# The scale half of layer 1's modulation is summed during the output projection of layer 0, not during the Hyena groups

## The chip, the cores and the metric

The kernel runs on one core of a Trainium2 chip. Its time is the device time of one execution in microseconds (us), and a version is compared by the median of several runs. TensorE (PE) multiplies, VectorE (DVE) and ScalarE (ACT) do elementwise work, GpSimd (POOL) does elementwise work and issues some DMAs, and SyncE's queue (SP) issues most DMAs. Each engine runs its own instructions strictly in the order in which they were written; a waiting instruction holds everything behind it.

## The reference

Two layers over 512 latent and 256 context tokens of width 1024. Each layer normalizes its input, applies a modulation that depends on a conditioning vector (shift, scale, gate), mixes and adds the gated result:

```
m = silu(c) @ ada_w[l] + ada_b[l]          # 3072 wide: shift, scale, gate
h = rms_norm(x, norm_g[l]) * (1 + scale) + shift
layer 0:  proj = h @ w_in;  u = x1 * v;  y = irfft(rfft(u) * rfft(k)) + u * d
          branch = (y * x0 * silu(z)) @ w_out      # 2048 channels, Hyena
layer 1:  branch = attention(h)                    # 16 query heads, 4 key heads
x = x + gate * branch
```

Latent tokens use the vector `c`, context tokens the vector `c_ctx`: the modulation is needed for two streams, numbered 0 and 1.

## The kernel before, in words

Layer 0 works on 8 groups g of two chunks of 128 channels. Per group, four convolutions per chunk (x1, v, z, x0) are matmuls whose fp32 weights arrive by DMA in a ring of three 512 KB buffers, tag `stg`; ACT splits off the high part `whi` (L121), POOL, or near the end DVE, the low part `wlo` (L122), and PE multiplies (L465 to L470). DVE turns the products in PSUM into the convolved rows `cvx` and `cvv` (L512 to L515); the pair of PSUM banks of a convolution is used again two convolutions later. Then come the transposed input `utl` (L543), spectra and their products `ab` (L560: `ab411a` is group 4, chunk 1, second part), whose reading of `pu` frees the PSUM bank in which PE next forms a lag of the next group's filter, `pk` (L379, L380; DVE takes it up at L382), and the inverse transform (`y`, L625 to L629, after ACT's `qs`, L624).

The modulation is a side job. `ada_pairs` makes five items for each 512 columns: four steps, each a 512 KB load `adas` (L189) into the same ring `stg` and one multiply-add per stream and half (L196 for the first, else L198) into the accumulators `adaacc`, and a last item that sums over partitions on PE and adds the bias (`adap`, L169 and L172), or for a gate writes rows. A list `todo` holds the items, and `ada_next` takes the next one. Its places: the letters `a` of `steps`, and two in the list handed to `x0_stage(g, 1, ...)`. These items stand as calls between the convolution's eight k steps, so that their position in each engine's order is fixed by the order in which the code is written.

After the groups comes layer 0's output projection in two halves of the 1024 output columns. `out_part(half, ...)` goes over 16 channel tiles `cht`: a weight pair every second tile (again `stg`, with `whi`/`wlo` or `whx`/`wlx`), the rows `yf` by a POOL DMA, split into `yh` (ACT) and `yl` (DVE, L752), and 18 matmuls into six PSUM banks `po`. `out_finish` adds the last two or four tiles, scales with the gate (`res`, L770) and so frees bank g of the six, which the other half needs next. `tables` loads a rope table into `stg` (`ropeq`, `ropek`, L809), multiplies it on POOL (L818, L822) and writes it to DRAM (`t_scrq`, `t_scrk`, L823, by SP). `make_gsc(1)` forms layer 1's column scale from the scale half; its first use is `turn_rows`, after the second half's `out_finish`. Attention, from about 1000 us, ends the kernel.

Of the kernel before, what the change touches and what calls it, by code (L numbers as in the profile page):

```python
# [11 lines left out]
F32 = mybir.dt.float32  # L12
F32R = mybir.dt.float32r
# [6 lines left out]
P = 128  # L20
# [32 lines left out]
def hybrid_kernel(ctx: ExitStack, tc: tile.TileContext, x, c, ctxt, c_ctx, norm_g, ada_w, ada_b,  # L53
# [20 lines left out]
    def f(ap):  # L74
        return ap.bitcast(F32)
# [99 lines left out]
    def make_gsc(l):  # L175
        for s in range(2):
            V.scalar_tensor_tensor(gsc[l][:, s * 8:(s + 1) * 8], ada[l][:, s * 24 + 8: s * 24 + 16], 1.0,
                                   vb[:, l * 8:(l + 1) * 8], ALU.add, ALU.mult)

    def ada_pairs(l, o0, streams, accp):  # L180

        nm = f"_{l}_{o0}"
        accs = []

        def step(kk):
            st = wp.tile([P, 1024], F32, tag="stg", name=f"adas{nm}_{kk}", bufs=NST)
            sv = st.rearrange("p (k o) -> p k o", k=2)
            src = ada_w[l][kk * 2 * P:(kk + 1) * 2 * P, o0:o0 + 512]
            nc.sync.dma_start(sv, src.rearrange("(k p) o -> p k o", p=P))  # L189
            for n_, s in enumerate(streams):  # L190
                if kk == 0:
                    accs.append(accp.tile([P, 512], F32, tag="adaacc", name=f"adaacc{nm}_{s}", bufs=NACC))
                for k in range(2):
                    sc = sil[:, s * 8 + kk * 2 + k:s * 8 + kk * 2 + k + 1]
                    if kk == 0 and k == 0:
                        V.tensor_scalar(accs[n_], sv[:, k, :], sc, None, ALU.mult)  # L196
                    else:
                        V.scalar_tensor_tensor(accs[n_], sv[:, k, :], sc, accs[n_], ALU.mult, ALU.add)  # L198

        def gate_rows():  # L200
            st = wp.tile([P, 1024], F32, tag="stg", name=f"adag{nm}", bufs=NST)
            nc.sync.dma_start(st[0:1, 0:512], ada_b[l:l + 1, o0:o0 + 512])
            for n_, s in enumerate(streams):
                pt = axt(f"adag{nm}_{s}")
                TE.matmul(pt[0:1, :], ones[:, 0:1], accs[n_], start=True, stop=True)
                V.tensor_tensor(st[0:1, 512:1024], pt[0:1, :], st[0:1, 0:512], ALU.add)
                nc.sync.dma_start(g_scr[f"{l}{s}"][:, o0 - 2 * DM:o0 - 2 * DM + 512], st[0:1, 512:1024])

        last = gate_rows if o0 >= 2 * DM else lambda: ada_cols(l, o0, 512, accs, streams, nm)
        return [lambda kk=kk: step(kk) for kk in range(4)] + [last]  # L210
# [391 lines left out]
    def x0_stage(g, j, items):  # L602
        i = 2 * g + j
        x0 = conv(i, f"x0_{i}", items)
        V.tensor_tensor(x0, x0, szs0.pop(i), ALU.mult)
        gxs[i] = x0
# [24 lines left out]

    todo = []
    for l, o0, streams in ([(0, 2048 + o * 512, [0, 1]) for o in range(2)]
                           + [(1, o * 512, [0, 1]) for o in range(4)] + [(1, 2048 + o * 512, [0]) for o in range(2)]):
        todo += ada_pairs(l, o0, streams, hp)

    def ada_next():
        if todo:
            todo.pop(0)()
# [6 lines left out]
    def filter_items(g):  # L646
        if g >= 8:
            return []
        lags = []
        return [lambda: lags.extend(kfilter(g))] + [lambda i=i: lags[i]() for i in range(6)]  # L650
# [24 lines left out]
    for g in range(8):  # L675
        ks = [later(kdft, g, *k) for k in KSETS]
        kn = later(knorm, g)
        ya = [lambda: y_stage(g - 1, 0)] if g else []
        yb = [lambda: y_stage(g - 1, 1)] if g else []
        def slots(text):  # L680

            table = {"n": kn[0], "N": kn[1], "a": ada_next, "-": none, "y": lambda: [y() for y in ya],
                     "Y": lambda: [y() for y in yb]}
            for i in range(4):
                table["mpoc"[i]], table["MPOC"[i]] = ks[i]
            return [lambda w=w: [table[ch]() for ch in w] for w in text.split()]

        sl = [slots(text) for text in steps[g == 0]]
        ta = u_stage(g, 0, sl[0], sl[1])
        tb = u_stage(g, 1, sl[2], sl[3] + ta)  # L690
        if g == 0 and "u" in dbg:
            for j in range(2):
                nc.sync.dma_start(dbg["u"][j], us[j])
        z_stage(g, 0, sl[4] + tb)
        x0_stage(g, 0, spectra(g, 0))
        z_stage(g, 1, spectra(g, 1) + [none])
        x0_stage(g, 1, [none, ada_next] + filter_items(g + 1) + [ada_next])
    while todo:
        ada_next()
    make_gsc(1)  # L700
    p0.close()
    wp2 = ctx.enter_context(pool("wpipe2", side="right"))

# [142 lines left out]
    p1.close()  # L846
    p2 = ctx.enter_context(ExitStack())
    o2 = p2.enter_context(pool("rows"))
    out_part(0, range(EARLY, NCH), TA, {6: load_rows, 10: lambda: tables(at_q_g, "q")})
    for g in range(NG):  # L850
        out_finish(g, 0, TA)
    out_part(1, range(NCH), TB, {4: lambda: tab_.update(k=tables(at_k_g, "k"))})
    tabk = tab_["k"]
    load_half("k0", EH, 0, None, V)
    load_half("k0", EH, 1, more_w, G)
# [462 lines left out]
```

## Time and profile before

| | us |
|---|---|
| median of 3 runs | 1518.78 (1512.92 to 1520.66) |
| profiled execution | 1517.56 |
| its span in the trace | 1515.7, mean granted clock 0.983 |
| PE busy | 1455.5 (96%) |
| DVE busy | 1183.7 (78%) |
| ACT, POOL busy | 547.5 (36%), 513.9 (34%) |

The Hyena groups take about 60 to 840 us, layer 0's output projection 840 to 960, layer 1 the rest. A share of the whole span is a mean over these three. A row of the timeline tells when an instruction began and how long it took; a bracket at its end tells how long its engine stood idle before it and which instruction ended the wait. A row of the windows has, for each engine, its busy time in the stretch, then the granted TensorE clock as a part of 2.4 GHz, the DMA engines' busy share, and GB/s.

### The profile page before, as it was taken

To read this page: it belongs to the slowest core of one execution; us is meant where nothing else is said; L and a number is where in the kernel's file an instruction comes from. 1 tells how busy PE (TensorE), PEld (TensorE's weight loads), DVE (VectorE), ACT (ScalarE), POOL (GpSimd) and SP (SyncE) were. 2 spreads that over 40 slices of the span, in tenths; PEclk is the share of its full clock that TensorE was granted. 3 is DMA by queue.
4 is the path that set the end of the run, shared out by engine and by line. 5 is a ranking of instruction groups with operands and counts; after the bars stand their busy time and mean duration, and the time that the engine had idled before them with its cause. 6 is when DMAs were issued, how large, how long until landed. Compare 5 with 4: busy or idle time off the path is not lost.

```text
span 1515.7 us, 22866 instructions
## 1 busy us (share of the span) xinstructions
PE 1455.5 (96%) x8787; PEld 1263.9 (83%) x8787; DVE 1183.7 (78%) x2004; ACT 547.5 (36%) x1057; POOL 513.9 (34%) x449
## 2 busy tenths in 40 slices
PE   8998999989999999999999999999999999999998
PEld 1787987878878878789888787799998998998987
DVE  5769879889789888987969644575787878878886
ACT  3431322313223223223232334543545544544542
POOL 2462744626537354264464343121110000000005
PEclk9999999999999999999999999999999999999999
DMA  8612223232232232223233667246232212212111
GB/s 298 189 50 83 78 77 91 77 93 86 74 105 69 85 87 70 87 85 90 84 98 108 236 218 260 72 123 214 85 112 70 82 58 70 84 57 70 44 64 74
DMA packets 150783, 157.45 MB, mean 104 GB/s; under 512 B 6953, under 2 KB 122212, under 8 KB 150164
## 3 DMA queue, kind: packets, MB, share of 16 engines
q1 hardware_dynamic: 146324, 134.76, 28.7%
q0 software_dynamic: 4208, 20.72, 4.0%
q8 instruction: 69, 1.13, 0.3%
q10 hardware_dynamic: 144, 0.52, 0.1%
q14 instruction: 38, 0.31, 0.1%
HBM read 138.14 MB, written 17.84 MB: 103 GB/s over the span
## 4 chain that ended last, share of the span: by engine, by line
PE 60%; DVE 23%; issue 5%; POOL 5%; DMA 4%; ACT 2%; SPq 0%; POOLq 0%; ACTq 0%; DVEq 0%
PE po L70 4%; PE po L72 4%; PE po L71 4%; DVE adaacc L198 3%; PE et L1114 3%; DMA adas<-in_ada_w_dram 2%; PE px L70 2%; PE pz L70 2%; PE px L72 2%; PE pz L72 2%; PE px L71 2%; PE pz L71 2%; PE pq L70 2%; PE pq L72 2%; PE pq L71 2%
## 5 line engine op out<-in xcount | busy, mean ns | idle before, releaser
L122 POOL TENSOR_TENSOR wlo<-stg,whi 128x1024 fp32r<-128x1024 f32 x64 | 159.3, 2489 | 260.9 <-ACT whi L121 256.6
L121 ACT CAST whi<-stg 128x1024 fp32r<-128x1024 f32 x99 | 103.8, 1049 | 233.6 <-PE pcz L468 81.1
L873 POOL TENSOR_TENSOR r2q<-s2q,mhalf 128x2 f32<-128x2 f32 x32 | 23.4, 731 | 343.6 <-DVE s2q L871 332.4
L465 PE MATMUL plx<-h_hi,whi 128*128 128x512 f32 x248 | 104.1, 420 | 8.1 <-DVE cvx L515 8.1
L198 DVE SCALAR_TENSOR_TENSOR adaacc<-adas,sil,adaacc 128x512 f32<-128x512 f32 x98 | 102.8, 1053 | 10.9 <-DMA adas<-in_ada_w_dram 10.6
L1102 ACT ACTIVATE E<-sc,st 128x768 f32<-128x768 f32 x64 | 57.7, 902 | 126.9 <-DVE st L1100 114.1
L469 PE MATMUL plx<-h_hi,wlo 128*128 128x512 f32 x248 | 101.3, 409 | 0.0
L466 PE MATMUL plx<-h_lo,whi 128*128 128x512 f32 x248 | 101.3, 408 | 0.0
L467 PE MATMUL pcx<-hc_hi,whi 128*128 128x256 f32 x248 | 72.5, 292 | 4.7 <-DVE cvx L515 4.6
L1099 DVE TENSOR_REDUCE st<-sc 128x1 f32<-128x768 f32 x64 | 61.0, 953 | 17.5 <-PE sc L72 17.2
L468 PE MATMUL pcx<-hc_lo,whi 128*128 128x256 f32 x248 | 71.7, 289 | 0.0
L470 PE MATMUL pcx<-hc_hi,wlo 128*128 128x256 f32 x248 | 71.5, 288 | 0.0
L752 DVE TENSOR_TENSOR yl<-yf,yh 128x768 fp32r<-128x768 f32 x26 | 25.7, 990 | 51.9 <-ACT yh L751 51.8
L1119 DVE TENSOR_TENSOR ptl<-et,pth 128x768 fp32r<-128x768 f32 x64 | 61.1, 954 | 5.3 <-ACT pth L1118 4.0
L465 PEld LDWEIGHTS plx<-h_hi,whi 128*128 128x128 f32 x248 | 49.2, 198 | 18.7 <-issue 8.8
L467 PEld LDWEIGHTS pcx<-hc_hi,whi 128*128 128x128 f32 x248 | 49.2, 198 | 18.5 <-issue 4.9
L1118 ACT CAST pth<-et 128x768 fp32r<-128x768 f32 x64 | 51.1, 798 | 31.1 <-PE et L1114 31.0
L468 PEld LDWEIGHTS pcx<-hc_lo,whi 128*128 128x128 f32 x248 | 49.1, 198 | 11.3
L465 PE MATMUL plv<-h_hi,whi 128*128 128x512 f32 x120 | 49.4, 412 | 5.5 <-DVE cvv L515 5.5
L72 PE MATMUL po<-pth,kvt 128*128 128x256 f32 x192 | 54.1, 282 | 0.0
L71 PE MATMUL po<-ptl,kvt 128*128 128x256 f32 x192 | 54.0, 281 | 0.0
L70 PE MATMUL po<-pth,kvt 128*128 128x256 f32 x192 | 53.9, 281 | 0.0
(909 smaller groups left out, 5181.5 us busy)
## 6 DMA issues: line engine op xcount, KB each, us to landing
stg<-in_hy_w_in_dram SPq DMA_DIRECT2D x64, 512.0 KB
stg<-in_at_w_in_dram SPq DMA_DIRECT2D x40, 512.0 KB
adas<-in_ada_w_dram SPq DMA_DIRECT2D x32, 512.0 KB
yf<-y_scr POOLq DMA_DIRECT2D x32, 384.0 KB, 5.0
ad<-in_ada_w_dram SPq DMA_DIRECT2D x16, 512.0 KB
stg<-in_hy_w_out_dram SPq DMA_DIRECT2D x16, 512.0 KB
stg<-in_at_w_out_dram SPq DMA_DIRECT2D x16, 512.0 KB
dec<-in_k_dec_dram SPq DMA_DIRECT2D x48, 128.0 KB
```

What stands on the lines that cost most here:

```text
L70: TE.matmul(ps, lh, rh, start=first, stop=False)
L71: TE.matmul(ps, lh, rl, start=False, stop=False)
L72: TE.matmul(ps, ll, rh, start=False, stop=last)
L121: S.copy(hi, st)
L122: (lo_eng or lo_default[0]).tensor_tensor(lo, st, f(hi), ALU.subtract)
L198: V.scalar_tensor_tensor(accs[n_], sv[:, k, :], sc, accs[n_], ALU.mult, ALU.add)
L465: TE.matmul(pl, hi[:, k, :], h_hi[:, k, :], start=fi, stop=False)
L466: TE.matmul(pl, hi[:, k, :], h_lo[:, k, :], start=False, stop=False)
L467: TE.matmul(pc[:, 0:LC], hi[:, k, :], hc_hi[:, k, :], start=fi, stop=False)
L468: TE.matmul(pc[:, 0:LC], hi[:, k, :], hc_lo[:, k, :], start=False, stop=False)
L469: TE.matmul(pl, lo[:, k, :], h_hi[:, k, :], start=False, stop=la)
L470: TE.matmul(pc[:, 0:LC], lo[:, k, :], hc_hi[:, k, :], start=False, stop=la)
```

## The change

The ten items of layer 1's columns 1024 to 2047 (the scale) leave the list that the Hyena groups work off. The first of the two places in `x0_stage(g, 1, ...)` goes, and with it the filter's items move one place earlier there. The ten items are put into `todo` again after the groups: two are taken in the first half of the output projection, after tiles 12 and 14, eight in the second, after tiles 0 to 3 and 5 to 8. Their accumulators lie in another pool's buffer of three (`kst`). `make_gsc(1)` comes after them.

```diff
--- before.py
+++ after.py
@@ -189,7 +189,7 @@
                 if kk == 0:
-                    accs.append(accp.tile([P, 512], F32, tag="adaacc", name=f"adaacc{nm}_{s}", bufs=NACC))
+                    accs.append(accp(f"adaacc{nm}_{s}"))
@@ -631,8 +631,8 @@
     for l, o0, streams in ([(0, 2048 + o * 512, [0, 1]) for o in range(2)]
-                           + [(1, o * 512, [0, 1]) for o in range(4)] + [(1, 2048 + o * 512, [0]) for o in range(2)]):
-        todo += ada_pairs(l, o0, streams, hp)
+                           + [(1, o * 512, [0, 1]) for o in range(2)] + [(1, 2048 + o * 512, [0]) for o in range(2)]):
+        todo += ada_pairs(l, o0, streams, lambda n: hp.tile([P, 512], F32, tag="adaacc", name=n, bufs=NACC))
@@ -694,10 +694,9 @@
         z_stage(g, 1, spectra(g, 1) + [none])
-        x0_stage(g, 1, [none, ada_next] + filter_items(g + 1) + [ada_next])
+        x0_stage(g, 1, [none] + filter_items(g + 1) + [ada_next])
     while todo:
         ada_next()
-    make_gsc(1)
@@ -846,10 +845,17 @@
-    out_part(0, range(EARLY, NCH), TA, {6: load_rows, 10: lambda: tables(at_q_g, "q")})
+    for o in range(2, 4):
+        todo += ada_pairs(1, o * 512, [0, 1], lambda n: f(o2.tile([P, 512], F32R, tag="kst", name=n, bufs=3)))
+    out_part(0, range(EARLY, NCH), TA, {6: load_rows, 10: lambda: tables(at_q_g, "q"), 12: ada_next, 14: ada_next})
     for g in range(NG):
         out_finish(g, 0, TA)
-    out_part(1, range(NCH), TB, {4: lambda: tab_.update(k=tables(at_k_g, "k"))})
+    late = {i: ada_next for i in range(12)}
+    late[4] = lambda: tab_.update(k=tables(at_k_g, "k"))
+    out_part(1, range(NCH), TB, late)
+    while todo:
+        ada_next()
+    make_gsc(1)
```

Three places show how the order moves. The first is DVE's order in group 4, from the second piece of `utl` on, before:

```order
L543 TENSOR_TENSOR utl_4304<-ut_4_4636,uth_4303 128x2x128
L198 SCALAR_TENSOR_TENSOR adaacc_1024_0_4599<-adas_1024_1_4871,sil,adaacc_1024_0_4599 128x512
L560 TENSOR_TENSOR ab400a<-pu_0_0_4664,kt_4454 128x1024
L198 SCALAR_TENSOR_TENSOR adaacc_1024_0_4599<-adas_1024_1_4871,sil,adaacc_1024_0_4599 128x512
L560 TENSOR_TENSOR ab400b<-pu_1_0_4677,kt4m_4217 128x1024
L198 SCALAR_TENSOR_TENSOR adaacc_1024_1_4602<-adas_1024_1_4871,sil,adaacc_1024_1_4602 128x512
L584 TENSOR_TENSOR ab400a<-ab400a,ab400b 128x1024
L198 SCALAR_TENSOR_TENSOR adaacc_1024_1_4602<-adas_1024_1_4871,sil,adaacc_1024_1_4602 128x512
L569 TENSOR_TENSOR Y_0_0_4695<-ab400a 128x256
```

The same stretch of DVE's order after the change, from four rows ahead of `utl`:

```order
L198 SCALAR_TENSOR_TENSOR adaacc_512_0_4530<-adas_512_2_4923,sil,adaacc_512_0_4530 128x512
L198 SCALAR_TENSOR_TENSOR adaacc_512_1_4533<-adas_512_2_4923,sil,adaacc_512_1_4533 128x512
L198 SCALAR_TENSOR_TENSOR adaacc_512_0_4530<-adas_512_2_4923,sil,adaacc_512_0_4530 128x512
L198 SCALAR_TENSOR_TENSOR adaacc_512_1_4533<-adas_512_2_4923,sil,adaacc_512_1_4533 128x512
L543 TENSOR_TENSOR utl_4273<-ut_0_4598,uth_4272 128x4x128
L543 TENSOR_TENSOR utl_4273<-ut_4_4605,uth_4272 128x2x128
L560 TENSOR_TENSOR ab400a<-pu_0_0_4633,kt_4428 128x1024
L560 TENSOR_TENSOR ab400b<-pu_1_0_4646,kt4m_4186 128x1024
L584 TENSOR_TENSOR ab400a<-ab400a,ab400b 128x1024
L569 TENSOR_TENSOR Y_0_0_4664<-ab400a 128x256
```

The multiply-adds that stood between the products now stand ahead of `utl`, all four of one step together; from `utl` to `ab411a` DVE's order holds six of them before and none after. Over the eight groups the number between `utl` and `ab{g}11a` goes from 4, 5, 5, 6, 6, 6, 4, 4 to 1, 3, 0, 0, 0, 2, 2, 0, and the number from there to the next group's first `cvx` from 4, 6, 6, 5, 5, 5, 2 to 4, 4, 4, 0, 4, 2, 2.

The second place is SP's order in the output projection, from the q table's gain on, before (`stg` with `in_hy_w_out` are weight pairs):

```order
L813 DMA tbk<-in_at_q_g_dram 128x128
L118 DMA stg_8126<-in_hy_w_out_dram 128x2x512
L823 DMA t_scrq<-tbk 128x1024
L118 DMA stg_8220<-in_hy_w_out_dram 128x2x512
L813 DMA tbk<-in_at_k_g_dram 128x128
L118 DMA stg_8274<-in_hy_w_out_dram 128x2x512
L118 DMA stg_8328<-in_hy_w_out_dram 128x2x512
L809 DMA ropek<-in_k_rope_dram 128x1024
L823 DMA t_scrk<-tbk 128x1024
L118 DMA stg_8398<-in_hy_w_out_dram 128x2x512
```

The same stretch of SP's order after, from the first modulation load on:

```order
L189 DMA adas_1024_0_8026<-in_ada_w_dram 128x2x512
L822 DMA t_scrq<-tbk 128x1024
L118 DMA stg_8058<-in_hy_w_out_dram 128x2x512
L189 DMA adas_1024_1_8070<-in_ada_w_dram 128x2x512
L118 DMA stg_8158<-in_hy_w_out_dram 128x2x512
L812 DMA tbk<-in_at_k_g_dram 128x128
L189 DMA adas_1024_2_8188<-in_ada_w_dram 128x2x512
L189 DMA adas_1024_3_8218<-in_ada_w_dram 128x2x512
L118 DMA stg_8224<-in_hy_w_out_dram 128x2x512
L189 DMA adas_1536_0_8289<-in_ada_w_dram 128x2x512
L118 DMA stg_8297<-in_hy_w_out_dram 128x2x512
```

Five loads through the ring now stand ahead of `ropek`, which with `t_scrk` follows directly on the last row, and the sixth, `adas_1536_1`, comes right behind `t_scrk`.

The third place is DVE's order where the first half's banks are freed (`res_0` to `res_5`), before:

```order
L770 TENSOR_TENSOR res_2_8172<-po_2_7636,gate_7889 128x512
L770 TENSOR_TENSOR res_3_8184<-po_3_7637,gate_7889 128x512
L770 TENSOR_TENSOR res_4_8196<-po_4_7638,gate_7889 128x512
L770 TENSOR_TENSOR res_5_8208<-po_5_7639,gate_7889 128x512
L752 TENSOR_TENSOR yl_3_8306<-yf_3_8304,yh_3_8305 128x768
```

The same stretch after:

```order
L769 TENSOR_TENSOR res_2_8110<-po_2_7560,gate_7813 128x512
L198 SCALAR_TENSOR_TENSOR adaacc_1536_0_8291<-adas_1536_1_8367,sil,adaacc_1536_0_8291 128x512
L769 TENSOR_TENSOR res_3_8122<-po_3_7561,gate_7813 128x512
L198 SCALAR_TENSOR_TENSOR adaacc_1536_0_8291<-adas_1536_1_8367,sil,adaacc_1536_0_8291 128x512
L769 TENSOR_TENSOR res_4_8134<-po_4_7562,gate_7813 128x512
L769 TENSOR_TENSOR res_5_8146<-po_5_7563,gate_7813 128x512
```

Two multiply-adds of the load `adas_1536_1` now stand ahead of `res_3` and `res_4`.

## Rows read from the trace of the kernel before

**Rows 1.** Windows: two stages (stretch; length; engines' busy us; PEclk; DMA; GB/s).
```profile
60.00:840.00 780.00, 735.12 (x4420) 646.02 (x4419) 667.27 (x892) 225.65 (x371) 388.80 (x285) 0.97 0.29 86
840.00:960.00 120.00, 119.02 (x538) 97.69 (x539) 55.32 (x60) 42.36 (x59) 39.27 (x61) 1.00 0.67 228
```
**Rows 2.** Waits of PE in 60 to 840 us: total, times, longest.
```profile
PE plx L465 <- DVE cvx L515: 8.1, 4, 2.7
PE plv L465 <- DVE cvv L515: 5.5, 5, 3.4
PE pcx L467 <- DVE cvx L515: 4.6, 2, 3.4
PE pk L379 <- DVE ab411a L560: 3.2, 1, 3.2
...
PE pk L379 <- DVE ab211a L560: 1.7, 1, 1.7
PE pu L71 <- DVE utl L543: 1.6, 1, 1.6
```
**Rows 3.** Timeline of PE: end of the first wait listed for `pk`.
```profile
535.86 0.64 PE L379 MATMUL pk<-w4h,h 128*128 128x512 f32 x1 [3.15 <-DVE ab411a L560]
```
**Rows 4.** Windows: PE right after four of these waits.
```profile
338.00:341.40 3.40, 3.38 (x18) 2.91 (x19) 3.40 (x5) 0.00 (x0) 0.00 (x0) 1.00 0.12 36
535.80:539.20 3.40, 3.34 (x10) 2.79 (x11) 3.40 (x5) 0.00 (x0) 0.00 (x0) 0.53 0.11 32
570.30:573.70 3.40, 3.31 (x11) 2.86 (x12) 3.40 (x5) 0.00 (x0) 0.00 (x0) 0.52 0.06 7
822.90:829.70 6.80, 6.25 (x21) 5.42 (x22) 6.76 (x8) 0.87 (x2) 3.02 (x2) 0.51 0.46 154
```
**Rows 5.** The instructions on L198 in 60 to 840 us: ns min/median/max.
```profile
L198 DVE SCALAR_TENSOR_TENSOR adaacc<-adas,sil,adaacc x98: 617/752/3377, 64.0 to 810.0; 128x512 f32<-128x512 f32 x98
```
**Rows 6.** Window with the instructions of L198 alone, group 4 (DVE busy us, count).
```profile
508.50:534.40 25.90, 6.40 (x6) 1.00 0.30 89
```
**Rows 7.** Timeline of DVE, groups 4 and 5.
```profile
507.55 1.02 DVE L543 TENSOR_TENSOR utl<-ut,uth 128x512 fp32r<-128x512 f32 x2 [2.51 <-ACT uth L542]
...
514.70 1.77 DVE L198 SCALAR_TENSOR_TENSOR adaacc<-adas,sil,adaacc 128x512 f32<-128x512 f32 x1
...
520.03 1.24 DVE L198 SCALAR_TENSOR_TENSOR adaacc<-adas,sil,adaacc 128x512 f32<-128x512 f32 x1 [0.62 <-DMA adas<-in_ada_w_dram]
...
534.50 1.21 DVE L560 TENSOR_TENSOR ab411a<-pu,kt4p 128x1024 f32<-128x1024 f32 x1
...
553.36 0.48 DVE L625 SCALAR_TENSOR_TENSOR y<-pq,rn,qs 128x256 f32<-128x256 f32 x1 [4.00 <-ACT qs L624]
...
564.74 3.80 DVE L395 TENSOR_REDUCE mx<-kfl 128x256 f32<-128x2048 f32 x1
...
570.16 0.47 DVE L515 SCALAR_TENSOR_TENSOR cvx<-pcx,vb,cvx 128x255 f32<-128x255 f32 x1
```
**Rows 8.** Timeline of SP and POOL, group 4.
```profile
513.85 2.08 POOL L369 TENSOR_TENSOR w4l<-w4s,w4h 128x512 fp32r<-128x512 f32 x1 [4.34 <-ACT w4h L368]
...
515.95 0.37 SPq L189 DMA_DIRECT2D adas<-in_ada_w_dram  x1
```
**Rows 9.** Windows: the output projection's busiest stretch of DMA.
```profile
856.00:877.00 21.00, 21.00 (x94) 17.25 (x93) 6.18 (x7) 5.92 (x7) 6.70 (x8) 1.00 0.97 350
```
**Rows 10.** Timeline of SP and POOL, output projection.
```profile
895.53 0.34 SPq L809 DMA_DIRECT2D ropek<-in_k_rope_dram  x1
...
900.96 0.62 POOL L818 TENSOR_TENSOR tbk<-ropek,tbk 128x128 f32<-128x128 f32 x1 [3.51 <-DMA ropek<-in_k_rope_dram]
...
906.91 0.34 SPq L823 DMA_DIRECT2D t_scrk<-tbk  x1
```
**Rows 11.** Timeline of DVE and PE, the second half's fourth bank.
```profile
909.82 0.69 DVE L770 TENSOR_TENSOR res<-po,gate 128x512 f32<-128x512 f32 x1 [3.18 <-POOL xr L771]
...
910.84 0.39 PE L70 MATMUL po<-whi,yh 128*128 128x512 f32 x1
```

## The prediction

> **What bounds the kernel now.** I read the windows by stage first. In the Hyena groups PE works 735.1 of 780 us and DVE 667.3, so neither is full and PE misses 44.9 us; in the output projection PE works 119.0 of 120 us, DVE only 55.3, and the DMA engines are busy for 0.67 of it [rows 1]. So PE is the clock of both stages, and what the change can win is PE's missing time in the first and what it can lose is new waits in the second. Next the waits of PE: nearly all name DVE [rows 2]. Seven are of `pk`, once in each of groups 0 to 6, for the product that frees its bank: 3.2, three of 3.1, 2.9, 2.6 and 1.7, together 19.7. Four are of L465 for `cvx`, 8.1, three of them about 2.65; one of L467, in the last group, 3.4; and those for `cvv` are 5.5. Third, the clock after such waits: in the 3.4 us after the waits that ended at 535.86 and 570.39 the granted clock was 0.53 and 0.52, the 1.2 GHz level for nearly all of them, after the wait of 1.7 it stayed at 1.00, and around the last group's wait it was 0.51 for 6.8 us [rows 3, 4]. A wait of 2.6 or more thus costs 3.4 x 0.47 = 1.6 us beside itself, the last 6.8 x 0.49 = 3.3.
>
> **What the change removes in the groups.** Ten items leave: eight loads with 32 multiply-adds on DVE (4 on L196, 28 on L198), and two column sums (`adap`). The sums, their tiny matmuls and two additions each go from one PE-bound stage to another and cost the same there: zero. The loads' own length doesn't count in the groups, where the DMA engines are busy for 0.29 [rows 1]; what matters is what stands in DVE's order ahead of `ab{g}11a` and of the next `cvx`.
>
> In group 4, six multiply-adds stand between `utl` and `ab411a`, 6.4 us in all, and DVE stood idle for at least 0.6 more for one load [rows 6, 7]. PE wanted the bank at 535.86 - 3.15 = 532.7; `ab411a` ended at 534.50 + 1.21 = 535.7 [rows 3, 7]. Without those 7.0 it ends at 528.7, and with `utl` 2.2 later (below) at 530.9: 1.8 ahead of PE. The other groups lose 3 to 6 of such instructions there, and only group 5, which keeps two, should keep a wait, about 0.8. So the seven waits of `pk` go, 19.7.
>
> The wait of L465 for `cvx` is the same kind of place: from 553.36, where `y` was released by `qs`, to 570.6 DVE worked without a gap, at 2.65 too late for PE [rows 2, 7]. After the change the three multiply-adds that stood there (2.3 at the median) are done ahead of `y`, and so is the long reduction `mx` of the filter, 3.80, because the filter's items moved one place earlier: both fill the 4.00 in which DVE waited for `qs`. The short `mx`, half its elements (1.9), comes in. That is 2.3 + 3.8 - 1.9 = 4.2 earlier against 2.65 needed. In groups 3 and 5 the order changes alike. These go: 8.1. So does the last group's 3.4, whose chain loses the same. With the clock, nine waits at 1.6 and one at 3.3, it is 17.7. Together 19.7 + 8.1 + 3.4 + 17.7 = 48.9, about the whole of what can be won.
>
> *A rule against it.* L198 took 617 ns at least, 752 at the median and up to 3377 [rows 5]; that at 514.70 took 1.77 while POOL's `w4l` ran from 513.85 to 515.93 [rows 7, 8]. The Trainium skill ("SBUF — State Buffer", section "Who interferes with whom") says that a DVE instruction with two SBUF inputs and a POOL instruction that reads SBUF exclude each other for the whole of one, whichever starts first. This trace agrees in that place. By that rule a blocked multiply-add that is taken away leaves its wait to the next two-input instruction, so that only 6 x 0.75 = 4.5 of the 6.4 come back; group 4 would have no slack left, and I estimate that half of the groups would keep a wait of 1 us: 4 us less.
>
> **What it adds in the groups.** With one place less per group the remaining items stand elsewhere. Ahead of `utl` in groups 3 and 4 (and 0) now stand all four multiply-adds of one step, whose load is issued on SP behind the filter's weights and waits for a ring slot. A load took 520.03 - 515.95 = 4.1 us to land [rows 7, 8]. DVE stood idle for 2.51 before `utl` [rows 7], so that 4 x 0.75 = 3.0 would nearly fit, but the load lands at about the time at which `utl` begins: `utl` starts 2.2 later in two groups and 0.8 in one by my walk through the order (bounds 0 and 3.0 each). Behind it wait `pu` on PE and all of DVE's products. I take 5.2, and 1.6 for the clock, as one of two such gaps would reach 2.6. In groups 0 to 2 three to four more multiply-adds stand ahead of the `cvv` that PE waits for; there the 5.5 stay, and I add 4 and 1.6. With the 0.8 of group 5 it is 5.2 + 1.6 + 4.0 + 1.6 + 0.8 = 13.2 (bounds 3 and 25). Net in the groups: -48.9 + 13.2 = -35.7, with bounds -46 and -20.
>
> **What it adds in the output projection.** DVE has room for the 32 multiply-adds, 24 us at the median beside 55.3 of 120 [rows 1, 5]; the loads are 4 MB more, and in the stretch 856 to 877 the DMA engines are already at 0.97 and 350 GB/s [rows 9]. The cost is one of order. The loads take turns in the ring of three with the weights and with `ropek`; five loads stand ahead of `ropek` and a sixth behind `t_scrk`. Before, `ropek` was issued at 895.53, POOL could begin its table at 900.96, and `t_scrk` was issued at 906.91, 5.9 later [rows 10]. Each of the five loads holds a slot for 4.1 of landing and 3.0 of its four multiply-adds, 7.1, and about two turn at a time: 5 x 7.1 / 2 = 18 later. So POOL begins at about 919, `t_scrk` goes at 925, `adas_1536_1` right after it, landing at 929; one multiply-add later (0.75) comes `res_3`, 0.69 long: 930.4. PE wants the bank of `res_3` at 910.84 [rows 11]. PE loses 19.6 there (smaller waits at `yl` before are inside that sum, since they delay PE to a place where it waits anyhow), and 1.6 by the clock: 21. Behind it nothing else is late: weights and rows for the next tiles are loaded meanwhile. The bounds: with three slots overlapping fully at the rate of 350 GB/s, 1.5 us per load, `ropek` is 7.5 later and the loss 9; with the loads one at a time, 35 later and 5.4 to land as `ropek` had, the loss is 38. I take 21, from the pace of the rows of single loads.
>
> **Sum.** 1517.56 - 35.7 + 21.2 = 1503.1; the runs' median lies 1.2 above the profiled execution, so 1504.
>
> **Rivals.** *The output projection hides it all.* If the ring turns faster than I say (DVE has 65 us of room there, rows 1), `res_3` isn't late, or late by less than 3: 1517.6 - 35.7 + 2 = 1484. For it speaks DVE's idle share; against it that `t_scrk` waits for POOL's table, which waits for the ring, and `res_3` stands behind both. Chance 0.2.
>
> *The relief doesn't reach PE.* If what ends the waits of `pk` is taken over by another release, `qs` of ACT (4.00 us before `y`, rows 7) or DVE's next chain, half of the 48.9 stays: the gain is 15 to 20 and the loss 21: 1517.6 - 17 + 21 = 1521, or with a smaller loss no change. For it: DVE is busy for 0.86 of the groups, and would be for as much after (667.3 - 24 of 780 - 35.7). Against it: the two places worked out above leave 1.8 and 1.5 us of slack. Chance 0.18, at 1515 to 1520.
>
> *The wait for `adas_1536_1` is the bigger term: slower.* One mechanism: SP's order behind `t_scrk`. If the five turns go one at a time, since each next load waits for multiply-adds that DVE may only do behind a `yl`, itself waiting for a DMA, `ropek` lands after 930, `res_3` comes at 945 and the loss is 34 + 1.6. It outweighs the groups' gain if that is at its lower part, 25: 1528. It decides from the point at which POOL's table for k begins after about 933. Chance 0.16.
>
> **How the numbers follow.** My forecast, 1491 to 1516, has 0.46. About 0.5% (7.6 us) is what a measurement of this kernel can tell from no change. Faster by more takes nine tenths of the forecast's 0.46 and the 0.2 of the first rival: 0.62. Within it lie the rest and most of the second: 0.19. Slower: 0.19. The range that leaves out a tenth on each side reaches to the first and the last rival: 1482 to 1528.
>
> **What would show it.** In the profile after, PE's waits for `ab{g}11a` should be gone, those for `cvx` gone from group 3 on, PE's clock in the groups 0.99 or more, and waits on `utl` of about 2 in groups 3 and 4. In the output projection there should be one wait of PE for `res` of 15 to 20 us, with SP's `t_scrk` and a load `adas` right before it. If that wait is missing, or if `pk` still waits, the forecast is wrong by that term.

## The result: slower by half a per cent

The changed kernel takes 1524.97 us (median of 8 runs, 1523.02 to 1527.48) against 1517.45 for the kernel before in the same series (1512.92 to 1521.39). The ratio is 1.0051, interval 1.0034 to 1.0068. The profiled execution's span is 1523.2 us, 7.5 more than the 1515.7 of before, so the two profiles can be compared stage by stage.

A place that both have is the first matmul of `po` with `whx` and `yh` (tile 3 of the first half). It stands at 855.1 before and at 835.2 after; the last of them at 979.1 and 986.2. So the groups and their tail became 19.9 us shorter, and the output projection 27.0 longer (124.0 before, 151.0 after); behind it the kernels differ by 0.4. The windows show the two stretches of the changed kernel (columns as in rows 1), to be read against [rows 1]:

```profile
60.00:840.00 780.00, 745.97 (x4512) 658.74 (x4512) 651.15 (x871) 232.72 (x383) 402.60 (x294) 0.98 0.29 86
835.20:986.20 151.00, 130.42 (x569) 105.14 (x568) 78.08 (x119) 47.67 (x72) 39.78 (x64) 0.93 0.59 199
```

In the output projection PE missed 2.0 us of 124 before (855.1 to 979.1); it now misses 20.6 of 151, at a granted clock of 0.93. The DMA engines are busy for 0.59 of it, against 0.61 in the same stretch before. That is a mean and doesn't say whether a single load came late. The waits of PE in 60 to 990 us name the places (total, times, longest), to be read against [rows 2]:

```profile
PE po L70 <- DVE res L769: 13.5, 2, 10.9
PE pu L71 <- DVE utl L543: 10.7, 3, 3.6
PE po L70 <- DVE cvx L515: 7.2, 1, 7.2
PE po L72 <- DVE yl L751: 5.4, 2, 4.0
PE plv L465 <- DVE cvv L515: 3.7, 2, 3.0
PE pk L379 <- DVE ab111a L560: 2.9, 1, 2.9
PE pk L379 <- DVE ab611a L560: 2.1, 1, 2.1
PE pk L379 <- DVE ab511a L560: 2.1, 1, 2.1
PE plz L465 <- DVE cvx L515: 1.3, 1, 1.3
```

The first and the fourth row are the output projection, 18.9 us, where there was 0.3 before. The rest are the groups: of the seven waits of `pk` (19.7) four are left (8.1 with one of 1.0), those for `cvx` at L465 and L467 have gone but for 1.5, and `utl` (1.6 before) and the last `cvx` (1.6 before) have grown.

The largest wait is the one that the prediction worked out. The timeline of SP, POOL, DVE and PE there (start, us, and in brackets idle time and what ended it), to be read against [rows 10, 11]:

```profile
895.85 0.34 SPq L808 DMA_DIRECT2D ropek<-in_k_rope_dram  x1
905.11 0.34 SPq L822 DMA_DIRECT2D t_scrk<-tbk  x1
905.54 0.39 SPq L189 DMA_DIRECT2D adas<-in_ada_w_dram  x1
```
```profile
901.18 0.45 POOL L817 TENSOR_TENSOR tbk<-ropek,tbk 128x128 f32<-128x128 f32 x1 [3.66 <-DMA ropek<-in_k_rope_dram]
```
```profile
911.09 0.75 DVE L198 SCALAR_TENSOR_TENSOR adaacc<-adas,sil,adaacc 128x512 f32<-128x512 f32 x1 [10.61 <-DMA adas<-in_ada_w_dram]
911.76 0.68 DVE L769 TENSOR_TENSOR res<-po,gate 128x512 f32<-128x512 f32 x1
```
```profile
912.50 0.80 PE L70 MATMUL po<-whi,yh 128*128 128x512 f32 x1 [10.90 <-DVE res L769]
```

With the groups 19.9 shorter, everything here would have come 19.9 earlier than before. `ropek` was issued 20.2 later than that (895.85 against 895.53 - 19.9), the table began 20.1 later, and the load behind the store held DVE for 10.61 us, with the release of PE's bank behind it.

The longest wait for `yl` stands behind a moved load too. ACT had the `yh` that this `yl` needs at 868.2, but in DVE's order four multiply-adds stood ahead of it, and DVE stood 8.01 us for their load (DVE, then PE):

```profile
873.36 2.74 DVE L198 SCALAR_TENSOR_TENSOR adaacc<-adas,sil,adaacc 128x512 f32<-128x512 f32 x4 [8.01 <-DMA adas<-in_ada_w_dram]
876.01 0.95 DVE L751 TENSOR_TENSOR yl<-yf,yh 128x768 fp32r<-128x768 f32 x1
```
```profile
877.02 0.52 PE L72 MATMUL po<-whi,yl 128*128 128x512 f32 x1 [4.03 <-DVE yl L751]
```

### The profile page after: what moved, and what is told of

Its sections match the earlier page's. It is cut to its first block, busy times and chain, and to the rows that moved or that the text cites. A ratio compares the mean times of both kernels' runs of the same rounds, so it can differ in the third digit from the quotient of the medians.

```text
span 1523.2 us, 22876 instructions
## 1 busy us (share of the span) xinstructions
PE 1454.5 (95%) x8787; PEld 1265.1 (83%) x8787; DVE 1173.5 (77%) x2004; ACT 548.0 (36%) x1057; POOL 516.4 (34%) x449
## 4 chain that ended last, share of the span: by engine, by line
PE 70%; DVE 14%; DMA 6%; POOL 4%; issue 3%; ACT 1%; SPq 0%; POOLq 0%; DVEq 0%; ACTq 0%
DMA adas<-in_ada_w_dram 4%; PE po L70 3%; PE et L1120 3%; PE po L72 3%; PE po L71 3%; DVE adaacc L198 3%; PE plx L465 2%; PE plx L466 2%; PE plx L469 2%; PE px L70 2%; PE pz L70 2%; PE px L72 2%; PE pz L72 2%; PE px L71 2%; PE pz L71 2%
## 5 line engine op out<-in xcount | busy, mean ns | idle before, releaser
L122 POOL TENSOR_TENSOR wlo<-stg,whi 128x1024 fp32r<-128x1024 f32 x64 | 165.5, 2586 | 225.8 <-ACT whi L121 225.6
L198 DVE SCALAR_TENSOR_TENSOR adaacc<-adas,sil,adaacc 128x512 f32<-128x512 f32 x98 | 93.6, 978 | 43.9 <-DMA adas<-in_ada_w_dram 43.5
L465 PE MATMUL plx<-h_hi,whi 128*128 128x512 f32 x248 | 101.5, 409 | 0.2 <-DVE cvx L515 0.2
L467 PE MATMUL pcx<-hc_hi,whi 128*128 128x256 f32 x248 | 70.6, 285 | 0.0
L467 PEld LDWEIGHTS pcx<-hc_hi,whi 128*128 128x128 f32 x248 | 47.6, 192 | 11.7 <-issue 0.2
L465 PEld LDWEIGHTS plx<-h_hi,whi 128*128 128x128 f32 x248 | 47.8, 193 | 10.1 <-ACT Fh3m L434 0.9
L121 ACT CAST whx<-stg 128x1024 fp32r<-128x1024 f32 x36 | 37.7, 1046 | 42.3 <-PE pz L71 16.1
L465 PE MATMUL plz<-h_hi,whi 128*128 128x512 f32 x128 | 51.6, 403 | 1.3 <-DVE cvx L515 1.3
```

The lines of the kernel that those rows point to most:

```text
L121: S.copy(hi, st)
L122: (lo_eng or lo_default[0]).tensor_tensor(lo, st, f(hi), ALU.subtract)
L465: TE.matmul(pl, hi[:, k, :], h_hi[:, k, :], start=fi, stop=False)
L467: TE.matmul(pc[:, 0:LC], hi[:, k, :], hc_hi[:, k, :], start=fi, stop=False)
```

## The experiments

Theory: the groups' gain and the output projection's loss are two terms that add; the loss is one of order (ring, SP's queue, DVE's queue), and the gain is smaller than forecast because DVE's late places are made in part by collisions with POOL (an instruction of one engine held up while one of the other runs), which don't go with the multiply-adds. Rivals: DMA rate; the loss as a consequence of beginning earlier; DVE late by its own work, such as the multiply-adds that stay in the groups and the wait for their loads.

### Each half alone

e1_groups_only leaves the ten items out altogether; layer 1's scale is formed from the shift's columns instead, so its output is not the reference's (a second edited line, in `make_gsc`, isn't shown).

```diff
-    for o in range(2, 4):
-        todo += ada_pairs(1, o * 512, [0, 1], lambda n: f(o2.tile(...)))
```

> The groups of the changed kernel with nothing put into the output projection: the scale half is left out and layer 1's scale is formed from the shift half, so the output is not the reference's. By the two profiles the groups and their tail end 20 us earlier than before (first PE work of output tile 3: 835.2 against 855.1). If the gain in the groups and the loss in the output projection are two separate terms, the time is about 1517 - 20 = 1497. If the wait of 7.2 us at the end of the groups is caused by loads that belong to the moved items, it is 1490 or less.

e2_out_only: before's list and places in the groups, and the output projection of the changed kernel.

```diff
+                           + [(1, o * 512, [0, 1]) for o in range(4)] + ...
+        x0_stage(g, 1, [none, ada_next] + filter_items(g + 1) + [ada_next])
```

> The groups of before with all forty items, and the ten items once more in the output projection as the changed kernel has them (the scale half is summed twice, the second result is used). Two separate terms: 1517 + 27 = 1544, with a wait of PE for the fourth bank of 9 to 12 us. If the output projection only suffers because it begins 28 us earlier and so meets the loads of rows and gates, the loss is under 15: 1530.

e1: 1497.64 us, ratio to before 0.9874 (0.9855 to 0.9892), 20.0 less. e2: 1545.42, ratio 1.0192 (1.0174 to 1.0211), 27.8 more. Their sum, 7.8, is the change's 7.5. So the terms are separate, each of the size read from the two profiles, and the loss does not come from beginning earlier: in e2 the groups end about as before (the place that was at 855.1 is at 856.2), and PE still waits 9.02 for the bank and 7.61 for `yl`:

```profile
901.59 0.80 PE L72 MATMUL po<-whi,yl 128*128 128x512 f32 x1 [7.61 <-DVE yl L751]
935.43 0.80 PE L70 MATMUL po<-whi,yh 128*128 128x512 f32 x1 [9.02 <-DVE res L769]
```

### What the output projection's loss is made of

e3_res_free keeps the five loads ahead of `ropek` and takes away the multiply-adds ahead of the bank's release.

```diff
-    late = {i: ada_next for i in range(12)}
+    late = {i: ada_next for i in (0, 1, 2, 3, 10, 11, 12, 13)}
```

> The changed kernel with the four late items of the scale half's second 512 columns taken at tiles 10 to 13 and not 5 to 8: five loads still go ahead of the rope table, but no multiply-add that needs the sixth load stands ahead of the bank's release. My theory, order behind the table's store: the wait of 10.9 for the fourth bank goes, with 2.6 of half clock behind it; the waits for yl (4.0, 1.4) stay: 1511. Rival, the DMA engines or the ring are simply too slow for the added 4 MB: PE waits elsewhere instead, 1520 to 1525.

1520.93, ratio 1.0023 (1.0007 to 1.0039): 4 less than the changed kernel, not 14. My expectation failed. The waits for `res` fell only from 13.5 to 7.0, those for `yl` rose from 5.4 to 7.9, and for `res` the trace says why. DVE and POOL of e3:

```profile
909.20 0.69 DVE L769 TENSOR_TENSOR res<-po,gate 128x512 f32<-128x512 f32 x1 [4.83 <-POOL xr L770]
```
```profile
903.42 0.45 POOL L817 TENSOR_TENSOR tbk<-ropek,tbk 128x128 f32<-128x128 f32 x1 [2.20 <-DMA ropek<-in_k_rope_dram]
...
907.90 7.45 POOL L770 TENSOR_TENSOR xr<-xr,res 128x512 f32<-128x512 f32 x6
```

The tile of `res` has three buffers. The fourth `res` waits for POOL's first addition to `xr`, and in POOL's order that stands behind the table, which waits for `ropek`. So the late `ropek` reaches the same bank by two ways, DVE's queue and POOL's, and e3 closed only one. The bracket of `res` before, 3.18 behind POOL's `xr` [rows 11], had shown the second way; I had not followed it.

f1_own_buffers takes the loads out of the ring, but not out of SP's order, and cuts each in two of 256 KB (unchanged lines are left out).

```diff
-            st = wp.tile([P, 1024], F32, tag="stg", name=f"adas{nm}_{kk}", bufs=NST)
+                sk = own(kk)          # own = lambda kk: xn[2 + kk]
+                for k in range(2):
+                    nc.sync.dma_start(sk[k], src[k * P:(k + 1) * P, :])
```

> The changed kernel, but the eight moved loads go into four buffers of their own (the tiles xn, which lie idle until the second half is finished, two 256 KB loads each) and not into the weight ring; same bytes, same places of the items, all eight loads still ahead of the rope table on SP. Theory, the ring's turns delay the rope table and with it POOL's table, the table's store and the bank releases: the waits for res and yl go, 1498 + 4 for the column sums = 1502. Rival, the DMA engines' rate (0.97 busy between 856 and 877 us before): the same bytes still delay rows and weights, PE waits for yl, 1512 to 1520.

1515.50, ratio 0.9983 (0.9969 to 0.9997): 9 less than the changed kernel, 13 more than I had expected, and a time that the rival gave. The projection lasts 140.3 (836.1 to 976.4) and not 151.0, so about 11 of the 27 go with the ring's turns. What stays, 16, is 3.7 of column sums (below), 6.2 of waits for `yl`, 3.0 for `res`, and about 3 that go with half clock (its granted clock is 0.98). `ropek` is issued at 887.56, still 11 later than before when both are counted from the projection's beginning, where it was 20 in the changed kernel. Whether those 11 are the DMA engines' rate (1.05 busy from 850 to 860 us in this trace) or the mere place of the loads in SP's and DVE's order, f1 does not show: it leaves the bytes and the places as they were.

e5_from_tile10 puts all ten items behind both.

```diff
-    out_part(0, ..., 12: ada_next, 14: ada_next})
+    out_part(0, ...})
-    late = {i: ada_next for i in range(12)}
+    late = {i: ada_next for i in range(10, 20)}
```

> All ten items from tile 10 of the second half on, four of them after the loop: no load of the scale half ahead of the rope table or the bank releases of the first half. My theory: no wait in the output projection but at its end, 1517 - 20 + 4 for the column sums = 1501. Rival: the last chain of load, multiply-add, column sum and scale is late for the transposed rows of layer 1 and the first weights of attention come late behind the loads: 1508 to 1515.

1508.09, ratio 0.9946 (0.9932 to 0.9961), the rival's number, and faster than before. The projection lasts 131.5 (839.2 to 970.7). PE's waits in 835 to 1000 us:

```profile
PE pk L70 <- DVE hc_hi L792: 2.4, 1, 2.4
PE adap L169 <- DVE adaacc L198: 1.7, 1, 1.7
PE x1T L789 <- ACT xr L778: 1.6, 1, 1.6
PE po L72 <- DVE yl L751: 1.3, 1, 1.3
```

No wait for `res` over 0.2 is left; the price has moved to the end, where column sums and layer 1's first rows come behind the last loads. In this execution, the longest of the seven, the projection is 7.5 longer than before, and what stands behind it, 541.1, is 4.5 longer. By the medians e5 lies 10.5 above e1, which has no scale half at all; the changed kernel lies 27 above it.

### Why the groups gave 20 and not 36

f2_filter_back puts the filter's items back by one place.

```diff
-        x0_stage(g, 1, [none] + filter_items(g + 1) + [ada_next])
+        x0_stage(g, 1, [none, none] + filter_items(g + 1) + [ada_next])
```

> As f1_own_buffers, and the filter's items one place later again in the last convolution of each group, where they stood before. The change moved them one place earlier, so that PE asks for the filter's bank 2.3 us earlier. If this earlier asking is why 8 us of waits for ab{g}11a stayed (2.9, 2.1, 2.1, 1.0), they fall under 2 in sum and the time is 6 to 9 below f1. If they stay because DVE is late by itself, nothing changes there, and the reduction mx moves back behind y, so that waits for cvx return: 0 to 5 above f1.

1514.16, ratio 0.9966 (0.9952 to 0.9979), 1.3 below f1, within the noise. The waits for ab111a, ab511a, ab611a are 2.9, 2.1, 2.1 as in f1. It excludes the place of the filter's items as their cause. The waits of L465 for `cvx` that I had expected back from the later `mx` didn't come either.

In the changed kernel the wait that ended for ab511a has this ahead of it on DVE, then on POOL:

```profile
615.42 1.21 DVE L584 TENSOR_TENSOR ab510a<-ab510a,ab510b 128x1024 f32<-128x1024 f32 x1
616.66 2.50 DVE L569 TENSOR_TENSOR Y<-ab510a 128x256 f32<-128x256 f32 x1
619.09 0.41 DVE L570 TENSOR_TENSOR Y<-ab510a 128x256 f32<-128x256 f32 x1
619.42 1.21 DVE L560 TENSOR_TENSOR ab511a<-pu,kt5p 128x1024 f32<-128x1024 f32 x1
```
```profile
614.86 4.02 POOL L122 TENSOR_TENSOR wlo<-stg,whi 128x1024 fp32r<-128x1024 f32 x1 [8.14 <-ACT whi L121]
```

Two instructions of the same shape, L569 and L570, take 2.50 and 0.41, and POOL's takes 4.02 where it takes 2.41 alone: each stood for the other. The 2.1 that DVE lost are as much as the 2.1 that PE then waited. But the collision isn't new. Before the change the same POOL instruction met `cvx` of L605, which takes 0.94 alone, in the same stretch (DVE, then POOL):

```profile
628.41 2.94 DVE L605 TENSOR_TENSOR cvx<-cvx,sz 128x768 f32<-128x768 f32 x1
```
```profile
628.13 2.41 POOL L122 TENSOR_TENSOR wlo<-stg,whi 128x1024 fp32r<-128x1024 f32 x1 [8.16 <-ACT whi L121]
```

And a second thing stands in that stretch of the changed kernel: the two multiply-adds that stay in group 5 come late, and DVE stands 2.48 us for their load, where it stood 0.94 in all for such loads before:

```profile
599.45 0.75 DVE L198 SCALAR_TENSOR_TENSOR adaacc<-adas,sil,adaacc 128x512 f32<-128x512 f32 x1 [2.48 <-DMA adas<-in_ada_w_dram]
```

f4 and g1 test the collision. No run takes away the kept multiply-adds alone.

f4_split_lo halves POOL's instruction.

```diff
-        (lo_eng or lo_default[0]).tensor_tensor(lo, st, f(hi), ALU.subtract)
+        for h0 in (0, 512):
+            (...).tensor_tensor(lo[:, h0:h0 + 512], st[:, h0:h0 + 512], f(hi)[:, h0:h0 + 512], ALU.subtract)
```

> As f1_own_buffers, and every low part of a weight is formed by two instructions of half the width. In the changed kernel a two-input instruction of DVE that met POOL's 2.4 us instruction took 2.5 instead of 0.41 (709.30, 616.66), as long as PE then waited for ab611a and ab511a (2.1, 2.1). If the whole instruction holds the port, halves give at most 1.2 and these waits shrink to about 1: 3 to 6 us below f1. If the two engines share it in smaller parts, the waits stay.

1509.61, ratio 0.9932 (0.9909 to 0.9954), 5.9 below f1, but not by the waits named, so that the time fell into the expected range by luck: they are 2.3 (ab511a), 2.3 (ab611a) and 2.9 (ab111a). DVE and POOL at the same place in f4:

```profile
613.96 1.40 DVE L576 TENSOR_TENSOR Y<-ab510a 128x256 f32<-128x256 f32 x1
615.28 1.49 DVE L577 TENSOR_TENSOR Y<-ab510a 128x256 f32<-128x256 f32 x1
```
```profile
612.01 4.47 POOL L123 TENSOR_TENSOR wlo<-stg,whi 128x512 fp32r<-128x512 f32 x2 [8.02 <-ACT whi L121]
```

Each of DVE's two now stands about 1.0 for one half (1.40 and 1.49 for 0.41). So here the engines took turns by instruction, and where DVE has several two-input instructions in a row, halving POOL's piece didn't lessen what it lost. What f4 gained lies elsewhere (`utl` 10.1 to 7.8, `cvv` 4.6 to 1.9, and the bank releases of the projection), and which of it is the halves' own effect I have not separated.

g1_lo_behind moves POOL's instruction behind the product.

```diff
+        if lo_behind is not None:                  # in load_w, on POOL, ahead of the low part
+            G.tensor_copy(lo[:, 0:1], lo_behind)
...
+        if name[3:] == "11a":                      # on DVE, behind the product
+            marks[int(name[2])] = gp.tile(...)
+            V.tensor_copy(marks[int(name[2])], t[:, 0:1])
```

> As f1_own_buffers, and POOL forms the low part of the next group's first weight only after DVE's product that frees the filter's bank (a one-column copy on DVE behind the product, and one on POOL ahead of the low part). In f1 that POOL instruction met DVE's two-input ones just ahead of ab511a and ab611a. Port theory: the waits for ab111a, ab511a and ab611a (2.9, 2.1, 2.1) fall under 1 each, with their half clock some 8 to 10 us: 1506. If DVE is late there by its own work, they stay and the time is that of f1, 1515.

The waits went as the port theory said (0.9, 0, 0), and the time did not: 1519.13, ratio 1.0004 (0.9985 to 1.0022). In its trace the sum behind the product takes 3.40 for 1.21, and PE's waits for `cvv` went from 4.6 in f1 to 12.9:

```profile
629.31 3.40 DVE L597 TENSOR_TENSOR ab511a<-ab511a,ab511b 128x1024 f32<-128x1024 f32 x1
```
```profile
PE plv L473 <- DVE cvv L525: 12.9, 4, 5.2
```

So the waits of groups 5 and 6 for the product need the collision: in g1 DVE still stands 2.50 for the load in group 5, and without the collision PE doesn't wait there. The kept multiply-adds have their part all the same. In f1 groups 0, 2 and 3, with one multiply-add or none between `utl` and the product but collisions of this size (a `Y` of 2.51 right ahead of the product and one of 2.59 to 2.64 earlier), leave waits of 0.9, 1.0 and 1.0; groups 5 and 6, with kept multiply-adds and one such collision, leave 2.1 each. That g1's moved collisions are also what makes the 8.3 more for `cvv` is argued from the order, not shown: its longest, 5.2 at 287.29, comes 43 us behind the moved collision of group 1, and in between DVE stands for two DMAs.

g2_best puts g1's edit beside e5's places; I had allowed that either theory might win.

```diff
+            G.tensor_copy(lo[:, 0:1], lo_behind)   # g1's order of POOL
-    late = {i: ada_next for i in range(12)}
+    late = {i: ada_next for i in range(10, 20)}    # e5's places
```

> The version to beat both: all items of the scale half from tile 10 of the second half on, as in e5_from_tile10 (1508), and the low part of the next group's first weight behind the product, as in g1. By the port theory 8 us below e5: 1500. If the port isn't the cause, 1508.

1514.26, ratio 0.9971 (0.9956 to 0.9986): 6 above e5 alone by the medians of two series, 4 by the ratios to the kernel before. It is a miss that says the same as g1:

```profile
PE plv L467 <- DVE cvv L519: 12.9, 4, 5.2
...
PE pk L381 <- DVE ab111a L564: 0.9, 1, 0.9
```

The wait for ab111a is short, that for `cvv` is 12.9 again, in the trace of another kernel: it is the edit that makes it.

f3_tail_order aims at the 7.2 at the end of the groups.

```diff
+                                         behind=last_act[0] if (half, cht) in ((0, 4), (0, 6)) else None)
```

> As f1_own_buffers, and ACT splits the output weights of tiles 4 and 6 only after the last convolution's rows. In the changed kernel ACT stood 10.7 us for such a weight at the end of the groups with the last convolution's step queued behind it. If that is the wait of PE at the end (7.2 for cvx), it falls to 2 or less, 4 to 5 us below f1. If DVE's own chain is the bound there (products, port), the wait stays at 5 to 7.

1513.85, ratio 0.9971 (0.9949 to 0.9992), level with f1. ACT now does the convolution's step in time, and the wait is 5.6 (5.7 in f1): the second branch. DVE's products ahead of it are the bound, again beside POOL:

```profile
796.72 2.87 DVE L596 TENSOR_TENSOR ab710a<-ab710a,ab710b 128x1024 f32<-128x1024 f32 x1
799.62 2.51 DVE L581 TENSOR_TENSOR Y<-ab710a 128x256 f32<-128x256 f32 x1
802.05 2.62 DVE L582 TENSOR_TENSOR Y<-ab710a 128x256 f32<-128x256 f32 x1
...
808.23 2.48 DVE L581 TENSOR_TENSOR Y<-ab711a 128x256 f32<-128x256 f32 x1
```

These four take 10.5 and alone take 1.2 and three times 0.4: 8 us lost beside POOL's rows and weights of the projection, which the tail begins with. That is read from the trace; no run takes these collisions away.

g4_utl_first takes the multiply-adds from ahead of `utl`.

```diff
-        z_stage(g, 0, sl[4] + tb)
+        z_stage(g, 0, tb + sl[4])
```

> As f1_own_buffers, and the transposes of the group's second chunk (ut, utl) stand ahead of the two modulation items of that stage instead of behind them, so that utl has no multiply-add ahead of it in groups 0, 3 and 4; four then stand between utl and the product that frees the filter's bank. Theory, PE's waits for utl (10.1 in three) come from the multiply-adds and their late load ahead of it: they go; but in groups 0, 3 and 4 the waits for ab{g}11a come back at 1 to 3 each: 0 to 6 us below f1. If utl is late by the input of ACT, nothing changes.

1508.01, ratio 0.9940 (0.9919 to 0.9961), 7.5 below f1 by the medians of two series, 6.5 by the ratios. The waits for `utl` are gone (10.1 in three), and those for ab011a, ab311a and ab411a have come back at 2.2 each, 4.7 more than in f1. With new waits of 3.1 for `ut` and 1.4 more for `cvv`, and smaller ones that fell, PE's waits up to the end of the groups are 5 less in all. What the rest of the gain is has not been separated.

### A version that beats both

h_best: e5's places, g4's order, f4's halves.

> Three edits that helped, together: the scale half from tile 10 of the second half on (e5: 1508), the second chunk's transposes ahead of the modulation items (g4: 7.5 below f1), the low parts in two halves (f4: 6 below f1). If the three take away separate waits, 1508 - 7.5 - 6 = 1495. If what they take away is one and the same shortage of DVE beside POOL in the groups, they don't add: 1500 to 1505.

1496.48 us, ratio 0.9870 (0.9842 to 0.9897): the three gains add, but for 1 or 2 us that lie in the noise. In 60 to 780 us its granted clock is 1.00, against 0.97 in the same stretch before (before, then h_best):

```profile
60.00:780.00 720.00, 679.52 (x4109) 598.94 (x4109) 617.85 (x830) 207.53 (x344) 362.08 (x268) 0.97 0.28 84
60.00:780.00 720.00, 697.55 (x4300) 616.22 (x4299) 610.63 (x836) 217.54 (x361) 401.95 (x338) 1.00 0.28 84
```

## Why the prediction was wrong

The prediction was 1504 with 1482 to 1528; the time, 1525, is inside the range but on the other side: I forecast faster with 0.62, and it is slower. The step that failed is the net in the groups, -35.7 predicted, -19.9 measured, -20.0 alone in e1; and in it first the removal, "So the seven waits of `pk` go, 19.7", with the clock that hangs on it.

*The removal in the groups.* Of the 19.7, 8.1 stayed. I had worked the step out in group 4 and carried it to the others with "The other groups lose 3 to 6 of such instructions there, and only group 5, which keeps two, should keep a wait". The counts that stand ahead of the prediction say otherwise: groups 1 and 6 lose only two, and groups 1, 5 and 6 keep three, two and two. Those are the three groups whose waits stayed at over 2 us. Each cell has the value before and after, in us; the stretch runs from the end of `utl` to the start of the product `ab{g}11a`:

| group | multiply-adds in the stretch | stretch | DVE idle for their loads | PE's wait |
|---|---|---|---|---|
| 4 | 6, 0 | 25.9, 21.3 | 0.9, 0 | 3.2, 0 |
| 1 | 5, 3 | 25.9, 25.7 | 0, 1.1 | 3.1, 2.9 |
| 5 | 6, 2 | 25.9, 24.9 | 0.9, 2.5 | 3.1, 2.1 |
| 6 | 4, 2 | 25.4, 24.9 | 1.0, 2.5 | 2.6, 2.1 |

In group 4 the step held, as in groups 0 and 3. In groups 1, 5 and 6 two things stood in the stretch that the prediction's sum had at nothing: the idle time for the kept loads, and DVE's collision with POOL's `wlo`, 2.0 us before and 2.0 to 2.1 after. In groups 0, 3 and 4 that collision is gone after the change; in group 2, which keeps no multiply-add, two such collisions stand in the stretch (2.64 and 2.51 for 0.41), with a wait of 1.0. g1 showed that the waits in groups 1, 5 and 6 fall to 0.9, 0 and 0 without it.

That a DVE instruction and POOL's held each other up for as long as the other ran is what the rows show (2.50 for 0.41 beside 4.02 for 2.41). The Trainium skill ("SBUF — State Buffer", section "Who interferes with whom") states the same for a DVE instruction with two SBUF inputs and a POOL instruction that reads SBUF. My own inference from it, priced at 4 us, that a multiply-add that goes leaves its collision to the next instruction, is not what happened in groups 1, 5 and 6: there the collision was on `cvx` before, as shown above, and simply stayed. One row fits it, in the last group: a multiply-add of 3.38 at 809.97 before, a `Y` of 2.50 at 788.67 after.

"So does the last group's 3.4": that one went, but the projection's first matmul of `po`, which waited 1.6 for the last `cvx` before, now waits 7.2. In the trace of f3 DVE's chain ahead of that `cvx` has 8 us of collisions. The waits of L465 for `cvx` went as worked out, from 8.1 to 0.2 for `plx`, with 1.3 new for `plz`.

*The addition in the groups.* `utl` came to 10.7 from 1.6, 9.1 more, where I took 5.2; the places (groups 0, 3, 4) and the mechanism, a late load with four multiply-adds ahead of `utl`, were right:

```profile
498.44 3.78 DVE L198 SCALAR_TENSOR_TENSOR adaacc<-adas,sil,adaacc 128x512 f32<-128x512 f32 x4 [3.36 <-DMA adas<-in_ada_w_dram]
502.14 1.01 DVE L543 TENSOR_TENSOR utl<-ut,uth 128x512 fp32r<-128x512 f32 x2
```

The waits for `cvv` were better than I took, 3.7 for 9.5.

*The clock.* I counted 17.7 back and 3.2 lost. Waits fell by 11.6 (all waits of PE to the end of the tail: 45.3 before, 33.7 after), the two column sums left with 2 x 1.84 of PE's time, and 4.6 of the 19.9 remain for the clock. Before, the 3.4 us behind eleven waits of 2.6 and more were at the 1.2 GHz level for part of the time (0.50 to 0.71); after the change eight such stretches are left, behind waits of 2.1 and more (0.50 to 0.73), as these two:

```profile
502.90:506.30 3.40, 3.40 (x13) 3.11 (x14) 1.48 (x2) 0.00 (x0) 0.00 (x0) 0.50 0.61 175
713.40:716.80 3.40, 3.38 (x10) 2.82 (x11) 3.40 (x5) 0.00 (x0) 0.00 (x0) 0.52 0.44 157
```

Where a wait only became shorter, 2.61 to 2.13 for ab611a, the stretch behind it was no better (0.53 before, 0.52 after). Nor is one price per wait right, as I had it with 1.6: in f1, behind two waits of 3.57 for `utl`, the next 3.4 us were at 1.00 (from 408.6) and at 0.50 (from 503.2). Sum of the misses: 9.6 of waits and 9.9 of clock, less 3.7 of column sums, is 15.8.

*The output projection.* The mechanism was right in its main steps: five loads ahead of `ropek`, 20 later where I worked out 18, the store, the sixth load, and PE's wait for the fourth bank. PE's waits are 18.9 in all where I took 19.6. That the 18 came so near is partly luck: I had put all of it on the ring's turns, and in f1, without them, 11 of the 20 stay. The term was 27.0 and not 21.2: 3.7 of column sums, which I had set at zero for both stages together, and about 5 of half clock where I took 1.6. The longest wait, 10.9, alone has this behind it:

```profile
912.50:916.00 3.50, 3.50 (x8) 2.67 (x9) 2.04 (x4) 1.72 (x4) 3.47 (x3) 0.50 0.20 75
```

And I had named one way from `ropek` to the bank; the trace of e3 shows a second, by POOL.

*The rivals.* "The relief doesn't reach PE" is the nearest (17 in the groups, 21 lost, 1521); it had 0.18. Of its two conditions it was not `qs` but DVE's own chain, by the kept loads and the collisions. The groups' -19.9 stands just outside their bounds, -46 to -20, and the output projection's, 9 to 38, held 27. That the range held the time has no more merit than that.

One sentence ahead of the prediction was too simple: the order isn't that of the calls alone. An item called at tile 5 of the second half stands, in the order shown, ahead of `res_3` of the first. With the items from tile 10 on, as in e5, hardly a wait for `res` is left; tiles between were not tried.

## What to carry to other kernels

A side job moved from a stage where it is in the way to one with idle engines pays in the order of the queues there: look for what stands behind its loads (here a store on SP, a table on POOL and `yl` on DVE) before counting idle time. A gain that was worked out in one of several like groups holds for the others only where the same instructions leave; list for each what stays, with the wait for its load and the collisions with another engine, which the removed instructions don't take along. And follow every bracket that a releasing instruction has in the trace before, not only the one that the change adds.

## What the runs showed of the hardware

POOL's 128x1024 subtraction and DVE's two-input instructions stood for one another for whole instructions: a 128x256 one of DVE took 2.50 for 0.41 and POOL's 4.02 for 2.41 where they met, and two took 1.40 and 1.49 beside two halves. Delaying POOL's instruction until after the product (g1) put the loss on DVE's next sum (3.40 for 1.21). With the short waits of the groups made fewer and shorter, the clock in 60 to 780 us went from 0.97 to 1.00 in h_best.
